# A LayerNorm's mean summed while the convolutions still run, its squares and rstd listed earlier

## The chip, the cores and the metric

The kernel runs on one core of a Trainium2 chip. The metric is the device time of one execution in microseconds (us); lower is better. A core has five engines that run side by side, each through its own fixed list of instructions in order: TensorE (PE, the matmuls; PEld is its weight load), VectorE (DVE), ScalarE (ACT), GpSimd (POOL) and SyncE (SP, which here only issues DMAs).

## The reference, cut to what matters

One layer of a hybrid block, 1024 tokens by 1024 channels, float32. The part that the change touches is mixer B, between the input projection and the merge:

```python
proj = jnp.einsum('bsd,de->bse', h, w_in[l])
b_s, c_s, v_s, v_c, gl_c, gate_br = jnp.split(proj, SPLITS[:-1], axis=-1)
y_a = b_s * causal_dwconv(c_s * v_s, conv_short_w[l])          # mixer A, width 3
y_a = jnp.einsum('bsc,cd->bsd', y_a, w_short_out[l])
u = v_c * jax.nn.sigmoid(gl_c)                                 # mixer B
u = causal_dwconv(u, conv_conf_w[l]) + conv_conf_b[l]          # width 31
u = jax.nn.silu(layer_norm(u, conf_ln_g[l], conf_ln_b[l]))     # mean and variance over channels
y_b = jnp.einsum('bsc,cd->bsd', u, w_conf_out[l])
```

and `layer_norm` is `(u - mean) * rsqrt(mean((u - mean)^2) + 1e-5) * g + b`. Gates, the output projection, a gated feed-forward part and the norms around them follow.

## The kernel before, in words

**Layout.** Activations lie transposed: 8 chunks of 128 channels on the partitions, 1024 tokens along the row, worked on in two halves of 512 (`halves`). A norm over channels is thus a sum over the 8 chunks (elementwise adds) and then a matmul with a 128x128 tile of ones, which sums over the partitions and puts the sum on all of them.

**Precision.** Every matmul operand is split into a high part (`wh`, `zsh`, `q00h`: a cast on ACT) and a low part (`wl`, `zsl`: a subtraction), and `mm3` issues three matmuls for each. The `wl` of the input projection and of `w_short` is made on POOL, that of most others on DVE. PE can only begin a block of weights when its `wl` is there.

**The stages around the change**, in the order of the program text:

1. The input projection ("win stage" below): 12 groups ("duals") of seven products each in the order of `PRODUCTS = "1265734"`. Each product fills PSUM banks named x, y or z, which DVE (`plus`, line 503; `minus_times`, line 507) and ACT read out. `u` chunks, the inputs of the wide convolution, come out of these. The products of the short convolution (`short_conv`, L494 to L496) go through `q_store` (casts `qs` on ACT at L487, subtraction on POOL at L488) to DRAM and come back with `q_load` (L580, SP) in the last dual.
2. The wide convolution `conv(j)`, 8 chunks, all on DVE: two differences (L595, L596), then 46 taps (L604) into two PSUM banks, and ACT's two L617 that add the bias and write the result back over `u[j]`. L618 stores the chunk to `cv_dram`. The calls stand after the win stage in the text, but each tap is tied by `tc.issue_after` to a certain read of a product, so that the convolutions run between the win stage's reads.
3. `y_a`: 8 blocks j of 48 matmuls (`ya`, `col_block`), each read by DVE (L675, which multiplies by a gate that POOL's DMA at L673 fetches), and each followed by one `modulation`, a 128x1024 product-and-sum on DVE (L258) of a row block of `w_ada` that SP loads. After block 1 the text has `ln_mean` and `ln_squares`: the 8 chunks are loaded again (L626, SP), summed on DVE (L628), scaled by 1/1024 (L629), multiplied by ones (`mu`, L632), copied (L633); then per chunk the mean is subtracted (L639), ACT squares (L642), DVE sums (L646). After block 6 it has `ln_rstd`: for each half the `var` matmul (L653), then `rstd`: Ln and Exp on ACT (L323, L324) and a Newton step on DVE (L329 to L331).
4. `y_b`: `row_blocks` over the normalised chunks. `act_b` scales a chunk half (L686), applies Silu (L687), calls a `modulation`, and splits the result (`zsh` L304 on ACT, `zsl` L305 on DVE), which PE takes chunk by chunk.

**What sets the order.** Tiles come from pools with a fixed number of buffers: `uc` (8 wide ones: u, p, sc, qs, sig, cv), `t` (58 of 128x512), `gs` (6), raw weights (5), `wh` and `wl` (3 each), PSUM 6 and 2 banks. A planner turns the text into one fixed list for each engine, by its own estimate of when each instruction can go; among those ready it takes the one listed first. On the chip the lists are then run as they stand, each instruction waiting for its data and for its buffer to come free. An instruction that waits holds all behind it on its engine, a DMA that waits for a buffer holds all behind it on its queue.

Of the kernel before, what the change touches and what calls it, by code (L numbers as in the profile page):

```python
# [34 lines left out]
F32 = mybir.dt.float32  # L35
# [11 lines left out]
SK = 3  # L47
# [58 lines left out]
def block_kernel(ctx: ExitStack, tc: tile.TileContext, xT, c, vecs, ada, w_first, w_plain, w_duals,  # L106
# [41 lines left out]
    def g_tile(name):  # L148
        return gsp.tile([P, H], F32, tag="gs", name=name)
# [168 lines left out]

    def rstd_start(ss, eps, name, n=H, tile_of=g_tile):

        r, t = tile_of(name + "r")[:, :n], tile_of(name + "t")[:, :n]
        ss = ss[:, :n]
        nc.scalar.activation(t, ss, AF.Ln, bias=eps)  # L323
        exp = nc.scalar.activation(r, t, AF.Exp, scale=-0.5)  # L324
        return ss, eps, r, t, exp.ins

    def rstd_end(ss, eps, r, t, exp):

# [1 line left out]
        nc.vector.scalar_tensor_tensor(out=t, in0=ss, scalar=eps, in1=t, op0=ALU.add, op1=ALU.mult)  # L330
        nc.vector.scalar_tensor_tensor(out=r, in0=t, scalar=1.5, in1=r, op0=ALU.add, op1=ALU.mult)  # L331
        return r

    def rstd(*args):
        return rstd_end(*rstd_start(*args))

    def load_ln(ins):

# [170 lines left out]
    def win_evac(pairs):  # L509

        st = [{} for _ in pairs]

        def start(e, kind, j):
            if kind == "u":
                u.append(u_tile(j))
                e["b"] = [u[j][:, CK - 1 + h * H : CK - 1 + (h + 1) * H] for h in range(2)]
            elif kind == "p":
                e["p"] = uc_tile(f"p{j}", T + SK - 1)
                nc.gpsimd.memset(e["p"][:, : SK - 1], 0.0)  # L519
                e["b"] = [e["p"][:, SK - 1 + h * H : SK - 1 + (h + 1) * H] for h in range(2)]  # L520
            elif kind == "g":
                e["t"] = [uc_tile("sig", T) for _ in range(2)]
                e["b"], e["c"] = ([t[:, s] for s in halves] for t in e["t"])

        def evac(i, m, ps):
            kind, j, *rest = pairs[i]
            e = st[i]
            if m == "1":
                start(e, kind, j)
                if kind == "q":  # L530
                    e["b"] = [g_tile("m")]
            if m == "6" and kind == "q":
                e["b"].append(g_tile("v"))
            if m in "16":
                nc.scalar.copy(e["b"][m == "6"], ps)
            elif m in "23":
                h = m == "3"
                b = e["b"][h]
                plus(b, ps, b)
                if kind == "u" and h:  # L540
                    nc.vector.tensor_tensor(b, b, e["z"], ALU.mult)
                elif kind == "p" and h:
                    minus_times(b, e["z"], b)
                elif kind == "q":
                    nc.vector.tensor_tensor(sc[j][:, halves[h]], b, sc[j][:, halves[h]], ALU.mult)
                elif kind == "g":
                    nc.scalar.activation(b, b, AF.Sigmoid)
            elif m == "5":
                e["z"] = e["c"][1] if kind == "g" else g_tile("z")
                nc.scalar.copy(e["z"], ps)  # L550
            elif m == "7":
                plus(e["z"], ps, e["z"])
                if kind in "ug":
                    nc.scalar.activation(e["z"], e["z"], AF.Sigmoid, scale=-1.0)
                elif kind == "q":
                    minus_times(sc[j + 1][:, halves[1]], e["z"], sc[j + 1][:, halves[1]])
            else:
                if kind in "ug":
                    sig = e["c"][0] if kind == "g" else g_tile("sig")
                    nc.scalar.activation(sig, ps, AF.Sigmoid, scale=-1.0)  # L560
                if kind == "u":
                    nc.vector.tensor_tensor(e["b"][0], e["b"][0], sig, ALU.mult)
                elif kind == "p":
                    minus_times(e["b"][0], ps, e["b"][0])
                    short_conv(j, e["p"])
                elif kind == "q":
                    minus_times(sc[j + 1][:, halves[0]], ps, sc[j + 1][:, halves[0]])
                    for i in range(2):
                        q_store(j + i)
                else:  # L570
                    for g, t in zip((j, *rest), e["t"]):
                        nc.scalar.dma_start(gate_dram[g], t)
        return evac
# [15 lines left out]
    def conv(j):  # L589
# [26 lines left out]
        for i, a in enumerate((a0, a1)):  # L616
            nc.scalar.activation(eo[:, : H, i], a, AF.Identity, bias=col(V_CB, j))  # L617
        nc.scalar.dma_start(cv_dram[j], u[j][:, :T])  # L618

    cv = []  # L620

    def ln_mean():
        tot = diffp.tile([P, T + CK - 1], F32, tag="diff", name="tot")[:, :T]
        for j in range(KC):
            cv.append(uc_tile(f"cv{j}", T))
            nc.sync.dma_start(cv[j], cv_dram[j])  # L626
            if j:
                nc.vector.tensor_tensor(tot, tot if j > 1 else cv[0], cv[j], ALU.add)  # L628
        nc.vector.tensor_scalar(tot, tot, 1.0 / D, None, ALU.mult)  # L629
        for h in range(2):  # L630
            mps = ps_tile("mu")
            nc.tensor.matmul(mps, ones, tot[:, halves[h]], start=True, stop=True)  # L632
            nc.scalar.copy(tot[:, halves[h]], mps)  # L633
        return tot

    def ln_squares():
        sqs = [None, None]
        for j in range(KC):
            nc.vector.tensor_tensor(cv[j], cv[j], mu, ALU.subtract)  # L639
            for h in range(2):  # L640
                sq = g_tile("sq")
                nc.scalar.activation(sq, cv[j][:, halves[h]], AF.Square, scale=1.0 / 32.0)  # L642
                if j == 0:
                    sqs[h] = sq
                else:
                    nc.vector.tensor_tensor(sqs[h], sqs[h], sq, ALU.add)  # L646
        return sqs

    def ln_rstd(sqs):
        rl = []  # L650
        for h in range(2):
            vps = ps_tile("var")
            nc.tensor.matmul(vps, ones, sqs[h], start=True, stop=True)  # L653
            rl.append(rstd(vps, eps2, f"rl{h}"))
        return rl

    n_duals = len(PAIRS) // 2
    for d in range(n_duals):
# [11 lines left out]
    for j in range(KC):  # L670
        for h, ps in enumerate(col_block(next_w(), qT, (0, 1), "ya")):
            ga = g_tile("ga")
            nc.gpsimd.dma_start(ga, gate_dram["a", j][:, halves[h]])  # L673
            ma[j, h] = s_tile(f"ma{j}{h}")
            nc.vector.tensor_tensor(ma[j, h], ps, ga, ALU.mult)  # L675
        if j == 1:
            mu = ln_mean()
            sqs = ln_squares()
        if j == 6:
            rl = ln_rstd(sqs)  # L680
        modulation(16 + j)


    def act_b(k, h):
        z = cv[k][:, halves[h]]
        nc.vector.tensor_tensor(z, z, rl[h], ALU.mult)  # L686
        nc.scalar.activation(z, z, AF.Silu, bias=col(V_LNB, k), scale=col(V_LNG, k))  # L687
        modulation(24 + KC * h + k)
        return split(z, s_tile, "zs")

    mg = [[None, None] for _ in range(KC)]

# [397 lines left out]
```

## Time and profile before

| | us |
|---|---|
| median of 3 runs (lowest, highest) | 1544.36 (1543.83, 1546.57) |
| profiled execution, its own time | 1546.12 |
| profiled execution, span of its instructions | 1544.4 |

| engine | busy us in the span | share |
|---|---|---|
| PE | 1472.5 | 95% |
| DVE | 1187.2 | 77% |
| ACT | 639.6 | 41% |
| POOL | 575.9 | 37% |

A timeline row reads: start, duration, engine, line, operation, names written and read, count, and in brackets the engine's idle time before it and what ended that. A row "A <- B: t, n, m" of the waits says that A waited for B t us in all, n times, at most m us. A row of a table of windows gives each engine's busy time in that stretch, with the number of instructions, and then PEclk, the clock that TensorE was granted as a share of full speed, the DMA engines' busy share and GB/s. A row of the groups gives busy us and mean ns, then the idle time before. Buffer numbers are left out of names.

### The profile page before, as it was taken

How to read it: one execution, taken by the hardware profiler on the slowest of the kernel's cores; microseconds unless marked ns; L12 is line 12 of the kernel's file. 1: busy time of each engine (PE TensorE's matmuls, PEld its weight loads, DVE VectorE, ACT ScalarE, POOL GpSimd, SP SyncE). 2: the span in 40 equal slices, each digit the busy share in tenths (PEclk: the TensorE clock that was granted, in tenths of full speed). 3: DMA queues.
4: the chain of work that ended last, by engine and by line, in shares of the span. 5: the costliest groups of instructions: out<-in, count | busy, mean ns of one | idle time of the engine just before them, and what ended most of it. 6: DMA issues, size and time to landing. Idle time of an engine off the chain costs nothing.

```text
span 1544.4 us, 17865 instructions
## 1 busy us (share of the span) xinstructions
PE 1472.5 (95%) x6466; PEld 1208.6 (78%) x6466; DVE 1187.2 (77%) x1543; ACT 639.6 (41%) x896; POOL 575.9 (37%) x491
## 2 busy tenths in 40 slices
PE   5799999999999998989899989999999999999996
PEld 3588887888887887768788868888888888788885
DVE  7887899999998965656865798876767665677756
ACT  6563334333333342344334564444444443221235
POOL 1316778688768883310111101100100016445005
PEclk9999999999999999999999999999999999999998
DMA  9332214223222269455754428544444449999403
GB/s 369 143 100 75 95 55 164 68 96 109 96 82 95 92 230 386 144 184 164 243 191 166 164 82 258 191 150 150 151 150 156 156 151 348 349 308 274 125 14 110
DMA packets 88024, 256.16 MB, mean 166 GB/s; under 512 B 10112, under 2 KB 12288, under 8 KB 87936
## 3 DMA queue, kind: packets, MB, share of 16 engines
q1 hardware_dynamic: 47248, 147.01, 28.5%
q0 software_dynamic: 36944, 95.44, 19.1%
q10 hardware_dynamic: 3744, 12.58, 2.0%
q8 instruction: 50, 0.82, 0.2%
q14 instruction: 38, 0.31, 0.1%
HBM read 188.41 MB, written 66.58 MB: 165 GB/s over the span
## 4 chain that ended last, share of the span: by engine, by line
PE 47%; DVE 3%; issue 1%; ACT 0%; DVEq 0%; ACTq 0%
PE x L276 7%; PE x L273 7%; PE x L274 7%; PE z L273 4%; PE z L274 4%; PE z L276 4%; PE y L273 3%; PE y L276 2%; PE y L274 2%; PE mix L276 2%; PE mix L273 2%; PE mix L274 2%; PE yb L274 1%; PE yb L276 1%; PE yb L273 1%
## 5 line engine op out<-in xcount | busy, mean ns | idle before, releaser
L201 ACT CAST wh<-raw 128x1024 fp32r<-128x1024 f32 (+2 forms) x260 | 262.1, 1009 | 439.5 <-PE x L274 99.7
L202 POOL TENSOR_TENSOR wl<-raw,wh 128x1024 fp32r<-128x1024 f32 (+1 forms) x95 | 247.3, 2608 | 154.5 <-ACT wh L201 149.6
L202 DVE TENSOR_TENSOR wl<-raw,wh 128x1024 fp32r<-128x1024 f32 (+2 forms) x165 | 189.1, 1147 | 58.3 <-ACT wh L201 55.7
L604 DVE SCALAR_TENSOR_TENSOR c<-diff,vec,c 128x512 f32<-128x512 f32 x248 | 182.2, 749 | 3.9
L841 POOL DMA_DIRECT2D hid<-stage x71 | 37.8, 534 | 354.1 <-DVE stage L313 350.9
L273 PE MATMUL x<-th,wh 128*128 128x512 f32 x336 | 130.8, 389 | 0.0
L276 PE MATMUL x<-th,wl 128*128 128x512 f32 x336 | 130.7, 389 | 0.0
L274 PE MATMUL x<-tl,wh 128*128 128x512 f32 x336 | 130.7, 389 | 0.0
L604 DVE SCALAR_TENSOR_TENSOR c<-u,wsum,c 128x512 f32<-128x512 f32 x112 | 84.0, 750 | 2.0
L273 PE MATMUL x<-t2h,wh 128*128 128x512 f32 x184 | 73.8, 402 | 5.9 <-ACT wh L201 4.5
L276 PE MATMUL x<-t2h,wl 128*128 128x512 f32 x184 | 73.8, 402 | 4.7 <-POOL p L519 3.4
L274 PE MATMUL x<-t2l,wh 128*128 128x512 f32 x184 | 73.7, 401 | 0.1
L273 PEld LDWEIGHTS x<-th,wh 128*128 128x128 f32 x336 | 63.1, 188 | 13.2 <-issue 0.3
L274 PEld LDWEIGHTS x<-tl,wh 128*128 128x128 f32 x336 | 63.1, 188 | 13.2
L276 PEld LDWEIGHTS x<-th,wl 128*128 128x128 f32 x336 | 63.1, 188 | 13.1
L273 PE MATMUL z<-th,wh 128*128 128x512 f32 x168 | 65.4, 389 | 1.5 <-ACT wh L201 1.5
L258 DVE CUSTOM_DVE_ANT_0 raw<-raw,cs,vec 128x1024 f32<-128x1024 f32 x24 | 30.7, 1281 | 45.7 <-DMA raw<-in_ada 45.7
L276 PE MATMUL z<-th,wl 128*128 128x512 f32 x168 | 65.4, 389 | 0.0
L274 PE MATMUL z<-tl,wh 128*128 128x512 f32 x168 | 65.4, 389 | 0.0
L312 ACT CAST stage<-g 128x512 fp32r<-128x512 f32 x62 | 38.3, 620 | 56.5 <-DMA hid<-stage 29.3
L273 PE MATMUL yb<-zsh,wh 128*128 128x512 f32 x128 | 49.5, 400 | 10.4 <-ACT zsh L304 9.4
L313 DVE TENSOR_TENSOR stage<-g,stage 128x512 fp32r<-128x512 f32 x62 | 42.5, 688 | 20.0 <-ACT stage L312 20.0
(819 smaller groups left out, 4087.5 us busy)
## 6 DMA issues: line engine op xcount, KB each, us to landing
hid<-stage POOLq DMA_DIRECT2D x71, 512.0 KB, 4.3
raw<-in_w_fi SPq DMA_DIRECT2D x50, 512.0 KB, 4.3
raw<-in_w_duals SPq DMA_DIRECT2D x48, 512.0 KB, 3.5
th<-hid POOLq DMA_DIRECT2D x71, 256.0 KB, 6.1
tl<-hid POOLq DMA_DIRECT2D x71, 256.0 KB, 6.3
ada<-in_ada SPq DMA_DIRECT2D x24, 512.0 KB, 7.5
raw<-in_ada SPq DMA_DIRECT2D x24, 512.0 KB, 4.3
raw<-in_w_fo SPq DMA_DIRECT2D x24, 384.0 KB, 6.1
```

Of the source, the lines that this page charges most:

```text
L201: nc.scalar.copy(wh, raw)
L202: lo_engine.tensor_tensor(wl, raw, f32(wh), ALU.subtract)
L258: nc.vector.tensor_tensor_reduce(out=raw, in0=raw, in1=cs, scale=1.0, scalar=col(V_ADA, b), op0=ALU.mult, op1=ALU.add, accum_out=modc(b),)
L273: nc.tensor.matmul(ps, wh, xh, start=first, stop=False, skip_group_check=again)
L274: nc.tensor.matmul(ps, wh, xl, start=False, stop=False, skip_group_check=again)
L276: mm3.ins = nc.tensor.matmul(ps, wl, xh, start=False, stop=last, skip_group_check=again).ins
L312: nc.scalar.copy(hi, src)
L313: nc.vector.tensor_tensor(lo, src, f32(hi), ALU.subtract)
L604: nc.vector.scalar_tensor_tensor(out=out, in0=src[:, s : s + H], scalar=wt, in1=acc, op0=ALU.mult, op1=ALU.add)
L841: nc.gpsimd.dma_start(hid_dram[key], s)
```

## The change

The sum over chunks is no longer made from the reloaded chunks. Two accumulators `tot` of 128x512 are taken from pool `t` and cleared on POOL ahead of the win stage; each `conv(j)` ends with two DVE additions that add the finished chunk's halves to them. `ln_mean` is now only two matmuls with ones and two ACT copies that carry the factor 1/1024. The reloads of the chunks stand in `ln_squares`, whose subtraction goes by halves. `ln_mean` and `ln_squares` are listed after block 0 of `y_a` rather than block 1, `ln_rstd` after block 5 rather than block 6, and within `ln_rstd` both `var` matmuls come first, then both Ln, then both Exp. In `act_b` the split stands ahead of the `modulation`. The clearing of the two leading columns of `p` moves from POOL to DVE.

```diff
@@ -318,11 +318,14 @@
 
     def rstd_start(ss, eps, name, n=H, tile_of=g_tile):
 
-        r, t = tile_of(name + "r")[:, :n], tile_of(name + "t")[:, :n]
+        t = tile_of(name + "t")[:, :n]
         ss = ss[:, :n]
         nc.scalar.activation(t, ss, AF.Ln, bias=eps)
-        exp = nc.scalar.activation(r, t, AF.Exp, scale=-0.5)
-        return ss, eps, r, t, exp.ins
+        return ss, eps, *exp_half(t, name, n, tile_of)
+
+    def exp_half(t, name, n=H, tile_of=g_tile):
+        r = tile_of(name + "r")[:, :n]
+        return r, t, nc.scalar.activation(r, t, AF.Exp, scale=-0.5).ins
 
     def rstd_end(ss, eps, r, t, exp):
 
@@ -330,9 +333,6 @@
         nc.vector.scalar_tensor_tensor(out=t, in0=ss, scalar=eps, in1=t, op0=ALU.add, op1=ALU.mult)
         nc.vector.scalar_tensor_tensor(out=r, in0=t, scalar=1.5, in1=r, op0=ALU.add, op1=ALU.mult)
         return r
-
-    def rstd(*args):
-        return rstd_end(*rstd_start(*args))
 
     def load_ln(ins):
 
@@ -516,7 +516,7 @@
                 e["b"] = [u[j][:, CK - 1 + h * H : CK - 1 + (h + 1) * H] for h in range(2)]
             elif kind == "p":
                 e["p"] = uc_tile(f"p{j}", T + SK - 1)
-                nc.gpsimd.memset(e["p"][:, : SK - 1], 0.0)
+                nc.vector.memset(e["p"][:, : SK - 1], 0.0)
                 e["b"] = [e["p"][:, SK - 1 + h * H : SK - 1 + (h + 1) * H] for h in range(2)]
             elif kind == "g":
                 e["t"] = [uc_tile("sig", T) for _ in range(2)]
@@ -616,28 +616,30 @@
         for i, a in enumerate((a0, a1)):
             nc.scalar.activation(eo[:, : H, i], a, AF.Identity, bias=col(V_CB, j))
         nc.scalar.dma_start(cv_dram[j], u[j][:, :T])
+        for h in range(2):
+            nc.vector.tensor_tensor(tot[h], tot[h], u[j][:, halves[h]], ALU.add)
 
     cv = []
+    tot = [hl_tile(f"tot{h}", dt=F32) for h in range(2)]
+    for t in tot:
+        nc.gpsimd.memset(t, 0.0)
 
     def ln_mean():
-        tot = diffp.tile([P, T + CK - 1], F32, tag="diff", name="tot")[:, :T]
+        mu = []
+        for h in range(2):
+            mps = ps_tile("mu")
+            nc.tensor.matmul(mps, ones, tot[h], start=True, stop=True)
+            nc.scalar.activation(tot[h], mps, AF.Copy, scale=1.0 / D)
+            mu.append(tot[h])
+        return mu
+
+    def ln_squares():
+        sqs = [None, None]
         for j in range(KC):
             cv.append(uc_tile(f"cv{j}", T))
             nc.sync.dma_start(cv[j], cv_dram[j])
-            if j:
-                nc.vector.tensor_tensor(tot, tot if j > 1 else cv[0], cv[j], ALU.add)
-        nc.vector.tensor_scalar(tot, tot, 1.0 / D, None, ALU.mult)
-        for h in range(2):
-            mps = ps_tile("mu")
-            nc.tensor.matmul(mps, ones, tot[:, halves[h]], start=True, stop=True)
-            nc.scalar.copy(tot[:, halves[h]], mps)
-        return tot
-
-    def ln_squares():
-        sqs = [None, None]
-        for j in range(KC):
-            nc.vector.tensor_tensor(cv[j], cv[j], mu, ALU.subtract)
             for h in range(2):
+                nc.vector.tensor_tensor(cv[j][:, halves[h]], cv[j][:, halves[h]], mu[h], ALU.subtract)
                 sq = g_tile("sq")
                 nc.scalar.activation(sq, cv[j][:, halves[h]], AF.Square, scale=1.0 / 32.0)
                 if j == 0:
@@ -647,12 +649,14 @@
         return sqs
 
     def ln_rstd(sqs):
-        rl = []
+        vs, ts = [], []
         for h in range(2):
-            vps = ps_tile("var")
-            nc.tensor.matmul(vps, ones, sqs[h], start=True, stop=True)
-            rl.append(rstd(vps, eps2, f"rl{h}"))
-        return rl
+            vs.append(ps_tile("var"))
+            nc.tensor.matmul(vs[h], ones, sqs[h], start=True, stop=True)
+        for h in range(2):
+            ts.append(g_tile(f"rl{h}t"))
+            nc.scalar.activation(ts[h], vs[h], AF.Ln, bias=eps2)
+        return [rstd_end(vs[h], eps2, *exp_half(ts[h], f"rl{h}")) for h in range(2)]
 
     n_duals = len(PAIRS) // 2
     for d in range(n_duals):
@@ -673,10 +677,10 @@
             nc.gpsimd.dma_start(ga, gate_dram["a", j][:, halves[h]])
             ma[j, h] = s_tile(f"ma{j}{h}")
             nc.vector.tensor_tensor(ma[j, h], ps, ga, ALU.mult)
-        if j == 1:
+        if j == 0:
             mu = ln_mean()
             sqs = ln_squares()
-        if j == 6:
+        if j == 5:
             rl = ln_rstd(sqs)
         modulation(16 + j)
 
@@ -685,8 +689,9 @@
         z = cv[k][:, halves[h]]
         nc.vector.tensor_tensor(z, z, rl[h], ALU.mult)
         nc.scalar.activation(z, z, AF.Silu, bias=col(V_LNB, k), scale=col(V_LNG, k))
+        hl = split(z, s_tile, "zs")
         modulation(24 + KC * h + k)
-        return split(z, s_tile, "zs")
+        return hl
 
     mg = [[None, None] for _ in range(KC)]
 
```

## The prediction

> **What bounds the kernel now.** The page first, for the busiest engine.
>
> ```profile
> span 1544.4 us, 17865 instructions
> PE 1472.5 (95%) x6466; PEld 1208.6 (78%) x6466; DVE 1187.2 (77%) x1543; ACT 639.6 (41%) x896; POOL 575.9 (37%) x491
> ```
>
> PE is busy in 1472.5 of 1544.4 us, so an edit that removes no matmul can win at most the 71.9 us in which PE stands, plus what it loses at a lowered clock after standing. The next view is therefore PE's own waits, and of these the ones that the edited code can touch:
>
> ```profile
> PE yb L273 <- ACT zsh L304: 9.4, 2, 7.4
> PE mu L632 <- DVE tot L629: 4.8, 1, 4.8
> PE x L276 <- POOL p L519: 3.4, 1, 3.4
> ```
>
> The timeline shows the first two in place, one in the middle of `y_a` and one at its end:
>
> ```profile
> 588.18 16.15 SPq L626 DMA_DIRECT2D cv<-cv  x8
> 590.42 0.39 PE L273 MATMUL ya<-q00h,wh 128*128 128x512 f32 x1
> 601.30 0.39 PE L273 MATMUL ya<-q00h,wh 128*128 128x512 f32 x1
> 611.84 1.22 DVE L628 TENSOR_TENSOR tot<-tot,cv 128x1024 f32<-128x1024 f32 x1
> 614.18 2.82 DVE L629 TENSOR_SCALAR tot<-tot 128x1024 f32<-128x1024 f32 x1
> 617.14 3.49 PE L632 MATMUL mu<-tot,ones 128*128 128x512 f32 x4 [4.80 <-DVE tot L629]
> 674.92 1.88 PE L653 MATMUL var<-sq,ones 128*128 128x512 f32 x4
> 681.87 1.28 ACT L323 ACT_TABLE_LOAD   x1 [2.18 <-issue]
> 694.40 0.61 ACT L304 CAST zsh<-cv 128x512 fp32r<-128x512 f32 x1
> 695.06 2.08 PE L273 MATMUL yb<-zsh,wh 128*128 128x512 f32 x4 [7.37 <-ACT zsh L304]
> ```
>
> A block of `y_a` takes 601.30 - 590.42 = 10.88 us. After block 1 PE comes to `mu` at 612.3 and waits 4.80 us for the sum, whose chunks were still being loaded up to 604. After block 7 it waits 7.37 us for the first normalised chunk, because `var` was computed only one block earlier and the chain from there to `yb` took 695.06 - 674.92 = 20.1 us. Both waits are followed by a slower clock:
>
> ```profile
> 200.00:300.00 100.00, 98.97 (x437) 81.65 (x436) 96.85 (x125) 39.35 (x54) 76.51 (x35) 1.00 0.31 101
> 300.00:400.00 100.00, 100.00 (x443) 82.84 (x442) 96.20 (x120) 40.95 (x55) 83.43 (x39) 1.00 0.28 101
> 400.00:500.00 100.00, 96.15 (x411) 78.68 (x411) 91.81 (x119) 34.54 (x46) 70.08 (x33) 0.97 0.27 94
> 617.14:620.70 3.56, 3.56 (x6) 1.66 (x7) 3.47 (x6) 0.62 (x2) 0.00 (x0) 0.57 0.45 115
> 695.06:699.10 4.04, 4.04 (x10) 3.23 (x11) 4.04 (x6) 3.45 (x6) 0.72 (x2) 0.54 0.63 162
> ```
>
> In the last two rows PE works at 0.57 and 0.54 of its clock: 3.56 x 0.43 = 1.53 us and 4.04 x 0.46 = 1.86 us are lost there. The first three rows are the win stage, and the price of the change: DVE, fifth column, is busy 96.85, 96.20 and 91.81 of 100 us, and that is where the sums now go.
>
> **The change part by part.**
>
> *The mean.* The last of the eight convolutions ends 20 us before `y_a` begins, as the stores show, which follow one another at (569.6 - 189.9) / 7 = 54 us, and DVE stands for 10 us after it:
>
> ```profile
> L618 ACTq DMA_DIRECT2D cv<-u x8: 326/326/327, 189.9 to 569.6; - x8
> 577.07 0.69 DVE L503 TENSOR_TENSOR sig<-x,sig 128x512 f32<-128x512 f32 x1 [10.18 <-issue]
> ```
>
> So `tot` is there by about 575, and `mu` after block 0 finds it ready: gain 4.80 + 1.53 = 6.33 us. The two `mu` matmuls stay, and the factor 1/1024 rides on copies that were there already. DVE loses seven 1024-wide additions and L629 from `y_a`; that was on PE's path only through the wait just counted, so nothing more is added for it.
>
> *Squares.* Eight subtractions of 1.2 us become sixteen of about 0.6: nothing. They wait for `mu` and the reloads. The reloads stand earlier in the text by one block, past the weight and `ada` loads of that block on SP's queue, but they were issued from 588.18 already and then took 16.15 us because they waited for `uc` buffers; the buffers come free as before, so SP stays held until about 604, and the weights behind it are as late as before. The squares ended so:
>
> ```profile
> 620.67 0.59 ACT L633 COPY tot<-mu 128x512 f32<-128x512 f32 x1 [0.86 <-PE mu L632]
> 648.81 1.29 DVE L258 CUSTOM_DVE_ANT_0 raw<-raw,cs,vec 128x1024 f32<-128x1024 f32 x1 [6.59 <-DMA raw<-in_ada]
> 650.02 1.29 DVE L646 TENSOR_TENSOR sq<-sq 128x512 f32<-128x512 f32 x2
> ```
>
> that is, at 651.3, 30 us after `mu`'s copies. Counted from the last reload, some 5 us after its issue near 604, they now end near 640.
>
> *rstd.* `var` after block 5 leaves blocks 6 and 7, 21.8 us, to cover the chain of 20.1 us, and the chain is shorter: two of its four table loads go (1.28 us each), and so does the 2.18 us before the second Ln, as both Ln now follow one another. With about 15 us of chain against 21.8 the wait of 7.37 goes, with its clock: 9.23 us. Next late is the other wait of `yb` on `zsh`, 9.4 - 7.4 = 2.0 us, which lies later in the stage and is not counted as won. If the cover of two blocks were lost, this term is what is paid again.
>
> *Split ahead of `modulation`* moves 0.6 us of DVE forward of 1.3 us in a stage where both fit: nothing. *Two more tiles of `t`* during the win stage: 56 of 58 are held by operands, so the loads of `q` may come up to two tiles later, at 3 matmuls or 10.88 / 16 = 0.68 us each. *The clearing of `p`* goes off POOL and onto DVE.
>
> ```profile
> 584.09 0.32 SPq L580 DMA_DIRECT2D q71l<-q  x1
> L519 POOL MEMSET p<- x8: 95/101/104, 58.2 to 484.5; 128x2 f32 x8
> ```
>
> The last `q` was issued at 584.09 and is used at the end of block 0, 600: nothing. The clearing is 0.1 us eight times, small beside the lag counted next.
>
> Gain so far: 6.33 + 9.23 = 15.56 us.
>
> *The sixteen additions.* This is the cost, and the trace has no such addition. The nearest rows are DVE's other two-input operations, both inputs in SBUF, of this width:
>
> ```profile
> 638.60 2.49 DVE L646 TENSOR_TENSOR sq<-sq 128x512 f32<-128x512 f32 x4
> L595 DVE TENSOR_TENSOR diff<-u 128x527 f32<-128x527 f32 x8 | 9.2, 1153 | 0.1
> L596 DVE TENSOR_TENSOR diff<-u 128x526 f32<-128x526 f32 x8 | 10.5, 1312 | 0.0
> L562 DVE TENSOR_TENSOR u<-u,sig 128x512 f32<-128x512 f32 x5 | 10.5, 2096 | 0.0
> L562 DVE TENSOR_TENSOR u<-u,sig x5: 680/2875/2884, 209.5 to 518.8; 128x512 f32<-128x512 f32 x5
> ```
>
> Outside the win stage one takes 2.49 / 4 = 0.62 us; inside it 1.15 and 1.31 us on average, and at worst 2.88. I take 1.23, the mean of L595 and L596, since they too are two in a row on `u`, at the start of each convolution as the additions are at its end. Bounds: 0.62 and 2.88.
>
> By the Trainium skill, page "SBUF — State Buffer", section "Who interferes with whom", a DVE instruction with two SBUF inputs and a POOL instruction that reads SBUF exclude each other, and the second waits for the whole of the first. That speaks against moving additions to where POOL is busiest. Worked out with POOL busy about 0.77 of the time in operations of 2.4 us (an estimate from that page), an addition would cost 0.62 + 0.77 x 1.2 = 1.55 us, and the median would come out at 1538.5 instead of the 1535.3 below.
>
> What is late by it? DVE's lists leave it little to catch up in:
>
> ```profile
> 265.23 0.69 DVE L503 TENSOR_TENSOR z<-x,z 128x512 f32<-128x512 f32 x1 [1.95 <-PE x L276]
> 341.39 0.69 DVE L503 TENSOR_TENSOR z<-x,z 128x512 f32<-128x512 f32 x1 [2.06 <-PE x L276]
> 417.55 0.69 DVE L503 TENSOR_TENSOR z<-x,z 128x512 f32<-128x512 f32 x1 [1.74 <-PE x L276]
> 500.93 0.69 DVE L503 TENSOR_TENSOR z<-x,z 128x512 f32<-128x512 f32 x1 [6.28 <-PE x L276]
> ```
>
> At 54 us each from 189.9 on, five convolutions have ended by 417. Their ten additions take 12.3 us against 1.95 + 2.06 + 1.74 = 5.75, so DVE reaches the end of the sixth 6.5 us later than before. The last six additions lie ahead of or among 6.28 and 10.18 us of slack and are hidden. A late DVE does not stop PE by itself, but at one place it does so through a queue:
>
> ```profile
> 456.72 0.73 ACT L617 ACTIVATE u<-c,vec 128x512 f32<-128x512 f32 x1 [6.00 <-DVE c L604]
> 457.33 1.03 ACT L201 CAST wh<-raw 128x1024 fp32r<-128x1024 f32 x1
> 458.44 2.40 POOL L202 TENSOR_TENSOR wl<-raw,wh 128x1024 fp32r<-128x1024 f32 x1 [5.11 <-ACT wh L201]
> 482.22 2.35 POOL L202 TENSOR_TENSOR wl<-raw,wh 128x1024 fp32r<-128x1024 f32 x1
> 484.62 0.79 PE L276 MATMUL x<-t2h,wl 128*128 128x512 f32 x1 [3.36 <-POOL p L519]
> ```
>
> ACT waits for the sixth convolution's last tap; the weight cast behind it on ACT waits too; POOL waits for the cast and then works without a break to 484.57, where PE has waited 3.36 us for that `wl` (the page puts it to the clearing of `p`, which ran beside it at 484.5). What DVE is late at 456.7 is late at 484.6: cost 6.5 us. Bounds: at 0.62 an addition, 6.2 - 5.75 = 0.5 us; at 2.88, 28.8 - 5.75 = 23.0 us. The additions also wait for ACT's second L617, 0.73 us, which the planner can fill with the next convolution's differences.
>
> Sum: -15.56 + 6.5 = -9.1 us. The profiled execution of 1546.12 would become 1537.1; the median of the runs lies 1.76 lower, 1544.36, and becomes 1535.3.
>
> **The rivals.**
>
> *Full gain.* The additions fall where POOL is idle or are spread by the planner, and cost what they cost outside: -15.56 + 0.5, 1529.3. For it: POOL is idle a quarter of the win stage, and a wait of 1.74 to 2.06 us comes with every second dual. Against it: the averages of L595 and L596.
>
> *Slower, by the additions.* If each meets a POOL operation as three of the five L562 did, the ten cost 28.8 us and the lag at 456.7 is 23.0 us: -15.56 + 23.0 = +7.5, 1551.8. It decides from (15.56 + 5.75) / 10 = 2.13 us per addition. For it: the 2.88 itself, POOL at 83.43 of 100 us in one window, and that a second addition right behind a first would find POOL waiting. Against it: L595 and L596 are such pairs and stay at 1.2. The page named above makes this same mechanism.
>
> *The wait at the end of `y_a` comes back.* If the planner lists the squares or `var` later than the text suggests, or if the gate loads of L673, which share the six `gs` tiles with the squares, hold up `y_a`'s PSUM banks, 9.23 us return: -6.33 + 6.5, within 0.2 us of 1544.4. For it: the 6.59 us above, in which DVE waited on an `ada` load with squares left to sum. Against it: 17 us lie between 640 and `var` after block 5, at 590.4 + 6 x 10.88 + 1.3 for `mu` = 657.
>
> **How the numbers follow.** Forecast case, a gain of some 4 to 13 us: 0.50. Full gain 0.22. Return of the wait 0.08. Slower by the additions 0.20. A measurement of this kernel can tell about 0.2%, 3.1 us: faster is the first two, 0.72; same is the third, 0.08; slower 0.20. The range runs from 1527, the full gain and the 2.0 us of `yb`'s other wait, up to 1549, an addition of 2.6 us; beyond them lie about 2 in 10. The likeliest case alone spans 1531 to 1541.
>
> **What would show it.** Right: no wait before `mu` nor before the first `yb`, the clock at 1.00 in both places, two blocks between `var` and `yb`, table loads down by two, L628 and L629 gone, sixteen additions in the win stage of 0.7 to 2 us, and PE's wait for `wl` after the ninth dual longer than 3.36. Wrong: additions of over 2.1 us or PE waits in the win stage of over 20 us in all; or the end of `y_a` still waiting on `zsh`; or new waits of PE on DVE's reads, which this kernel does not have in the win stage.

## The result, and the profile after

| | before, us | after, us |
|---|---|---|
| median (lowest, highest) | 1544.09 (1543.37, 1546.57) | 1559.74 (1557.17, 1563.87) |
| span of the profiled execution | 1544.4 | 1558.7 |
| `y_a` begins | 590.4 | 599.8 |
| first `yb` matmul | 695.1 | 708.7 |

The changed kernel is slower: the ratio of the times is 1.0101, 95% interval 1.0076 to 1.0126. Forecast was 1535.3, a gain of 9.1 us. In the profiled executions 9.4 us are lost before `y_a` begins and another 4.3 from there to the first `yb`; `y_b` loses 3.3 more, and later stages give 2.7 back; these two were not followed further.

The page of the changed kernel, for the engines, and then PE's waits that the change can touch:

```profile
span 1558.7 us, 17886 instructions
PE 1480.1 (95%) x6466; PEld 1212.5 (78%) x6466; DVE 1203.5 (77%) x1567; ACT 635.3 (41%) x894; POOL 578.0 (37%) x485
```

```profile
PE yb L273 <- ACT zsh L304: 8.1, 2, 6.1
PE ya L273 <- DVE ma L679: 7.1, 2, 4.7
PE x L276 <- POOL wl L202: 4.0, 3, 1.8
```

PE does the same 6466 matmuls in 7.6 us more; its mean granted clock is 0.982 instead of 0.986. The wait for `mu` is gone. The wait before the first `yb` fell only from 7.37 to 6.14. In the win stage the waits of x for `wl` grew from 1.0 us, once, to 4.0 in three, and small waits for reads by ACT and DVE are new; new too is the wait of `y_a` for its own read-outs. The timeline of the changed kernel shows where, the win stage first:

```profile
223.89 0.50 PE L273 MATMUL x<-th,wh 128*128 128x512 f32 x1 [1.39 <-ACT v L535]
238.98 0.50 PE L273 MATMUL x<-th,wh 128*128 128x512 f32 x1 [1.19 <-DVE sig L503]
255.05 0.50 PE L276 MATMUL x<-t2h,wl 128*128 128x512 f32 x1 [1.69 <-POOL wl L202]
371.41 0.50 PE L276 MATMUL x<-t2h,wl 128*128 128x512 f32 x1 [1.79 <-POOL wl L202]
485.88 0.50 PE L276 MATMUL y<-h40h,wl 128*128 128x512 f32 x1 [1.34 <-POOL wl L202]
495.12 0.51 PE L276 MATMUL x<-t2h,wl 128*128 128x512 f32 x1 [3.50 <-POOL u L405]
```

The last of these is the wait of 3.36 us that the kernel before has at 484.62, hardly longer; the others were 1.03 us (the third), 0.5 (the fifth) or nothing there. Between 180 and 500 us PE waits 12.0 us instead of 4.9. Then `y_a` and the first `yb`:

```profile
599.79 0.39 PE L273 MATMUL ya<-q00h,wh 128*128 128x512 f32 x1
610.68 1.88 PE L631 MATMUL mu<-tot,ones 128*128 128x512 f32 x4
649.92 0.77 PE L273 MATMUL ya<-q00h,wh 128*128 128x512 f32 x1 [4.71 <-DVE ma L679]
678.83 0.47 PE L273 MATMUL ya<-q00h,wh 128*128 128x512 f32 x1 [2.36 <-DVE ma L679]
708.69 3.36 PE L273 MATMUL yb<-zsh,wh 128*128 128x512 f32 x7 [6.14 <-ACT zsh L304]
```

`mu` has no bracket: it found its input. A `ya` matmul that waits for `ma` waits for a PSUM bank: the halves of three blocks fill the six banks, and the fourth cannot begin before the first is read out. Each of the three bracketed waits here is followed by a stretch at half clock, PEclk 0.50 in this table of windows:

```profile
649.10:655.90 6.80, 5.98 (x14) 4.77 (x15) 6.06 (x9) 1.04 (x1) 5.68 (x6) 0.50 0.92 317
679.80:683.20 3.40, 3.40 (x10) 2.62 (x9) 0.16 (x1) 1.50 (x3) 0.00 (x0) 0.50 0.67 267
707.10:713.90 6.80, 5.21 (x12) 4.18 (x13) 5.17 (x9) 3.62 (x7) 0.90 (x2) 0.50 0.73 225
```

So up to the first `yb` the stage pays 4.71 + 2.36 in waits and about 3.0 + 1.7 in clock (half of what PE worked in the first two windows), and wins 6.33 at `mu` and 1.23 at `yb`: 11.8 - 7.6 = 4.2 us, about the loss seen.

### The profile page after: what moved, and what is told of

Its sections match the earlier page's. It is cut to its first block, busy times and chain, and to the rows that moved or that the text cites. A ratio compares the mean times of both kernels' runs of the same rounds, so it can differ in the third digit from the quotient of the medians.

```text
span 1558.7 us, 17886 instructions
## 1 busy us (share of the span) xinstructions
PE 1480.1 (95%) x6466; PEld 1212.5 (78%) x6466; DVE 1203.5 (77%) x1567; ACT 635.3 (41%) x894; POOL 578.0 (37%) x485
## 4 chain that ended last, share of the span: by engine, by line
PE 46%; DVE 3%; issue 1%; ACT 0%; DVEq 0%; ACTq 0%
PE x L276 7%; PE x L274 7%; PE x L273 7%; PE z L274 3%; PE z L273 3%; PE z L276 3%; PE y L273 2%; PE y L274 2%; PE y L276 2%; PE mix L276 2%; PE mix L273 2%; PE mix L274 2%; PE yb L273 1%; PE yb L274 1%; PE yb L276 1%
## 5 line engine op out<-in xcount | busy, mean ns | idle before, releaser
L276 PEld LDWEIGHTS x<-th,wl 128*128 128x128 f32 x336 | 63.1, 188 | 14.1 <-POOL wl L202 1.0
L258 DVE CUSTOM_DVE_ANT_0 raw<-raw,cs,vec 128x1024 f32<-128x1024 f32 x24 | 35.5, 1482 | 42.0 <-DMA raw<-in_ada 30.5
```

The source lines that it names most:

```text
L258: nc.vector.tensor_tensor_reduce(out=raw, in0=raw, in1=cs, scale=1.0, scalar=col(V_ADA, b), op0=ALU.mult, op1=ALU.add, accum_out=modc(b),)
L276: mm3.ins = nc.tensor.matmul(ps, wl, xh, start=False, stop=last, skip_group_check=again).ins
```

## The experiments

Three theories came out of the two traces. **A**: the additions make DVE late in the win stage, and with it ACT's casts, POOL's `wl` and PE. **B**: listing reloads and squares after block 0 keeps `y_a`'s read-outs waiting; at first I took the gate loads behind the squares' `gs` tiles as the cause. **C**: the wait before the first `yb` is not the rstd chain, but that the split takes its tile from pool `t`, whose tiles are handed out in the order of the text, so that it can't be placed ahead of the last `ma` of `y_a`. The rival to B and C is the prediction's own: the chain from `var` to `yb`. All times are medians; the kernel before ran beside each group at 1543.0 to 1543.9.

| run | edit | median, us | ratio to before (95%) | `y_a` begins | first `yb` |
|---|---|---|---|---|---|
| a_noadds | after, no additions | 1548.40 | 1.0033 (1.0020, 1.0045) | 590.0 | 698.7 |
| a_wide | after, wide additions | 1555.37 | 1.0077 (1.0057, 1.0096) | 595.8 | 703.9 |
| a_pooladds | after, additions on POOL | 1556.12 | 1.0080 (1.0065, 1.0095) | 596.9 | 706.8 |
| a_poolms | after, `p` cleared on POOL | 1562.77 | 1.0120 (1.0095, 1.0145) | 604.5 | 713.6 |
| a_sq1 | after, reloads and squares after block 1 | 1543.69 | 1.0003 (0.9987, 1.0020) | 598.4 | 692.9 |
| a_rel0 | after, squares alone after block 1 | 1557.00 | 1.0093 (1.0070, 1.0116) | 599.6 | 706.7 |
| a_sq1_r6 | a_sq1, rstd after block 6 | 1540.89 | 0.9984 (0.9974, 0.9993) | 599.2 | 692.2 |
| a_z0 | after, own tile for chunk 0's split | 1554.08 | 1.0061 (1.0039, 1.0084) | 599.7 | 701.6 |
| b_z0 | before, own tile | 1538.63 | 0.9973 (0.9958, 0.9988) | 590.9 | 689.2 |
| a_sq1_z0 | a_sq1, own tile | 1538.25 | 0.9965 (0.9954, 0.9976) | 597.5 | 688.0 |
| b_z0_j2 | b_z0, mean and squares after block 2 | 1532.92 | 0.9925 (0.9910, 0.9940) | 590.0 | 682.0 |
| n_sum2 | after without additions, and the findings | 1533.60 | 0.9930 (0.9913, 0.9947) | 589.0 | 681.9 |

**The additions (A).** The first run takes them out and leaves `tot` cleared.

```diff
-        for h in range(2):
-            nc.vector.tensor_tensor(tot[h], tot[h], u[j][:, halves[h]], ALU.add)
```

> After, without the sixteen additions: the accumulators keep their zeros, so the mean is left out of the LayerNorm. Theory A (the additions meet POOL's operations, 1.73 us each, DVE falls behind and PE pays in the win stage): y_a begins near 590 instead of 599.8, the stage's PE gaps shrink to those of before (1.0, 0.5, 3.4 us), and the time falls by about 9.5 us, to 1550. Rival (the planner's new order and the clearing of p on DVE cost it): y_a still begins near 599 and the time stays within 3 us of 1559.7. Neither expects y_a itself to change: 4.7, 2.4 and 6.1 us of gaps stay.

1548.4: 11.3 us come back, and `y_a` begins at 590.0, where the kernel before has 590.4. The additions are the cost of the win stage. Theory A named ACT's casts and POOL's `wl` as the way to PE; the lines above show waits for reads by ACT and DVE as well. The waits behind the win stage remain, `y_a`'s own (5.11 and 2.63 us) and the one before `yb`, which grew to 8.19 us, so the rest of the loss is another matter. Next, one addition of double width instead of two:

```diff
-        for h in range(2):
-            nc.vector.tensor_tensor(tot[h], tot[h], u[j][:, halves[h]], ALU.add)
+        nc.vector.tensor_tensor(totw, totw, u[j][:, :T], ALU.add)
```

> The changed kernel with one addition of 128x1024 at the end of each convolution instead of two of 128x512, on an accumulator of that width; since SBUF is full, the pool of 128x512 tiles has 57 buffers instead of 58. In the changed kernel an addition of 128x512 took 0.68 us at best and 1.73 on average, 2.90 at most. If the difference is a wait that each instruction pays once (for a POOL operation under way), a wide one takes 1.2 us of its own (L628 of before, 1.22) and about 1.05 of waiting, 2.3 in all, the first five 11.5 instead of 15.5, and y_a begins some 4 us sooner, near 596 us; the time falls by about 4 us, to 1555 or 1556. If DVE simply works at a lower rate there, a wide one takes 3.4 us and neither y_a's start nor the time moves. One tile of the pool less can cost up to some us elsewhere, so the start of y_a decides, not the median.

The groups of the changed kernel and of this one (busy us, mean ns), then their rows by tile (min/median/max ns):

```profile
L620 DVE TENSOR_TENSOR tot<-tot,u 128x512 f32<-128x512 f32 x16 | 27.2, 1730 | 0.8 <-ACT u L617 0.8
L620 DVE TENSOR_TENSOR tot<-tot,u x16: 675/2032/2898, 191.4 to 577.6; 128x512 f32<-128x512 f32 x16
```

```profile
L619 DVE TENSOR_TENSOR tot<-tot,u 128x1024 f32<-128x1024 f32 x8 | 14.0, 1756 | 0.8 <-ACT u L617 0.8
L619 DVE TENSOR_TENSOR tot<-tot,u x8: 1211/1222/2827, 192.9 to 572.3; 128x1024 f32<-128x1024 f32 x8
```

Twice the width takes the same mean time, the best case goes from 0.68 to 1.21, and five of the eight wide ones take no more than 1.23: what is paid above the work itself is a wait per instruction, not a lower rate. The timeline shows what is waited for. Each of the nine additions of the changed kernel that took over 1.7 us ends 0.55 us after the POOL instruction that was under way; the one of 2.28 us at 358.99, for example, after POOL's `wl` of 357.87 to 360.72. `y_a` begins 4.0 us sooner, as expected, and the median falls by 4.4. But the first five wide additions took 8.8 us, not the expected 11.5, against 15.5 for the ten narrow ones: of 6.8 us less on DVE only 4.0 arrive at `y_a`. Then the additions on POOL:

```diff
-            nc.vector.tensor_tensor(tot[h], tot[h], u[j][:, halves[h]], ALU.add)
+            nc.gpsimd.tensor_tensor(tot[h], tot[h], u[j][:, halves[h]], ALU.add)
```

> The changed kernel with the sixteen additions issued on POOL instead of DVE. POOL's own 128x512 subtraction with two inputs (L488) took 1.48 us on average in the win stage, so sixteen are some 22 us, on an engine that is busy about 78 of 100 us there. If what costs is only that DVE is late (lag at the sixth convolution, then ACT, the weight cast, POOL's wl and PE), the lag goes and POOL takes the additions into its idle time, but for one or two that fall into its stretch without a break at 458 to 484 us: y_a begins near 592 us and the time is near 1552. Rival: POOL's idle time is waiting for casts and no slack, each addition makes the wl behind it late by its length, and DVE's two-input operations wait for POOL instead: y_a begins at 600 us or later and the time is 1560 or more.

```profile
L620 POOL TENSOR_TENSOR tot<-tot,u 128x512 f32<-128x512 f32 x16 | 25.7, 1625 | 14.6 <-ACT u L617 14.6
```

Neither number was met: `y_a` begins at 596.9, between the two expectations. POOL carries 25.7 us of additions and stands 14.6 us ahead of them for ACT's L617; `y_a` begins 6.9 us later than without additions. Neither engine of the two has them for nothing. Last, the clearing of `p` back on POOL:

```diff
-                nc.vector.memset(e["p"][:, : SK - 1], 0.0)
+                nc.gpsimd.memset(e["p"][:, : SK - 1], 0.0)
```

> The changed kernel with the clearing of p back on POOL: this takes out that part alone. On DVE the eight clearings took 0.06 us each, one of them after a wait of 1.01 us for a DMA that stores a gate. Theory (the part costs nothing): 1558 to 1561, no difference that can be told. Rival (a clearing that waits on DVE for its buffer holds all behind it, just where DVE is late): 1 to 3 us faster, and the waits of PE near 255 and 371 us shorter.

```profile
L620 DVE TENSOR_TENSOR tot<-tot,u 128x512 f32<-128x512 f32 x16 | 31.6, 2005 | 0.8 <-ACT u L617 0.8
```

Against 27.2 us in the changed kernel: two more additions met a POOL operation (2.9 us instead of 0.68), and `y_a` begins 4.7 us later. The medians can't be told apart (1557.63 to 1566.06 here, 1557.17 to 1563.87 there). The price of an addition thus hangs on where in POOL's work it falls, which an edit of 0.06 us instructions moves by some us.

**Reloads and squares (B).** Both listed after block 1, the mean still after block 0:

```diff
         if j == 0:
             mu = ln_mean()
+        if j == 1:
             sqs = ln_squares()
```

> After, with the reloads and squares listed after block 1 of y_a again, the mean still after block 0. Theory B (the gate loads of block 1 stand behind the squares' tiles, so blocks 1 to 3 fill the six PSUM banks and block 4 waits): the gap of 4.71 us ahead of block 4 and the half clock behind it (3.0 us) go, the time falls by 5 to 8 us, to about 1553. Rival (POOL's slow weight operation of 10.8 us is what holds the banks, whatever the place of the squares): the gap stays at 3 us or more.

1543.69, 16 us less, twice what I had expected: both waits of `ya` went, with their half clocks, and the wait before `yb` fell to 3.68. The place in the text is what costs, but this edit moves two things. The last run parts them: the reloads stay after block 0, the squares alone go after block 1.

```diff
         if j == 0:
             mu = ln_mean()
+            ln_reload()
         if j == 1:
             sqs = ln_squares()
```

> The changed kernel with the squares listed after block 1 (as in the run in which reloads and squares were both listed there, 1543.69 us), but with the eight reloads still listed after block 0, as the changed kernel has them. This parts the two things that moved together: the reloads' place on SP's queue and the squares' place on DVE, ACT and POOL. If the reloads are the cause (ahead of one ada and one w_short load they hold SP until 615 us; DVE stands for the ada load, ACT for the weights, the second copy of mu comes at 622.9 and the squares begin at 621.9), the squares begin near 622 again, run without a break, PE waits for read-outs of y_a about 4 us or more, and the time is 1552 to 1560. If the squares' place is the cause (ahead of the gate loads and the read-out of block 1), the read-out of block 1 comes before them, PE finds banks, and the time is 1543 to 1547. Anything between 1547 and 1552 means that both count.

1557.0, `y_a`'s wait is 6.6 us, now in one piece, ahead of block 6, where the changed kernel has the second of its two:

```profile
635.57 1.28 DVE L682 TENSOR_TENSOR ma<-ya,ga 128x512 f32<-128x512 f32 x2
674.46 1.28 DVE L258 CUSTOM_DVE_ANT_0 raw<-raw,cs,vec 128x1024 f32<-128x1024 f32 x1 [3.52 <-DMA raw<-in_ada]
675.67 1.28 DVE L682 TENSOR_TENSOR ma<-ya,ga 128x512 f32<-128x512 f32 x2
676.50 0.77 PE L273 MATMUL ya<-q00h,wh 128*128 128x512 f32 x1 [6.63 <-DVE ma L682]
```

So about 13 of the 16 us are the reloads' place on SP's queue, and my first reading of B, the gate loads behind the squares, explains at most the other 2.7. What the reloads do in the changed kernel is in the timelines. Before:

```profile
584.77 1.32 SPq L189 DMA_DIRECT2D raw<-in_w_short  x2
586.15 0.42 SPq L189 DMA_DIRECT2D raw<-in_ada  x1
587.50 0.33 SPq L189 DMA_DIRECT2D raw<-in_w_short  x1
588.18 16.15 SPq L626 DMA_DIRECT2D cv<-cv  x8
604.39 0.43 SPq L189 DMA_DIRECT2D raw<-in_ada  x1
```

After:

```profile
595.48 1.18 SPq L189 DMA_DIRECT2D raw<-in_w_short  x2
598.17 16.79 SPq L640 DMA_DIRECT2D cv<-cv  x8
615.01 0.42 SPq L189 DMA_DIRECT2D raw<-in_ada  x1
615.49 0.42 SPq L189 DMA_DIRECT2D raw<-in_w_short  x1
...
620.72 1.29 DVE L258 CUSTOM_DVE_ANT_0 raw<-raw,cs,vec 128x1024 f32<-128x1024 f32 x1 [8.79 <-issue]
621.93 1.29 DVE L642 TENSOR_TENSOR cv<-cv,tot 128x512 f32<-128x512 f32 x2
621.96 1.05 ACT L201 CAST wh<-raw 128x1024 fp32r<-128x1024 f32 x1 [9.62 <-DMA raw<-in_w_short]
622.92 0.59 ACT L632 ACTIVATE tot<-mu 128x512 f32<-128x512 f32 x1
633.79 10.76 POOL L202 TENSOR_TENSOR wl<-raw,wh 128x1024 fp32r<-128x1024 f32 x1 [8.30 <-ACT wh L201]
644.49 2.15 POOL L677 DMA_DIRECT2D ga<-gate_a  x4
649.08 1.34 DVE L679 TENSOR_TENSOR ma<-ya,ga 128x512 f32<-128x512 f32 x2 [3.45 <-DMA ga<-gate_a]
```

One `ada` load and one weight load that stood ahead of the eight reloads stand behind them now, and the reloads hold SP for 16.79 us while `uc` buffers come free. DVE stands 8.79 us before a `modulation`, whose `ada` row was asked for only at 615.01 (the bracket says no more than "issue"), ACT 9.62 us at the cast of that weight, and the second copy of `mu` is listed behind the cast. So the squares begin at 621.93, though `mu` was multiplied at 610.68. They then run with one break of 0.3 us, DVE busy 20.08 of 20.40 us (621.9 to 642.3), nearly all two-input operations; POOL's next `wl`, 2.40 us elsewhere, takes 10.76 and ends 2.3 us after them; the gate load behind it on POOL goes out at 644.49, and block 1 is read out at 649.08, after PE has filled all banks. In a_sq1, with the two loads ahead again, the squares begin at 611.0, block 1 is read out in the midst of them, at 623.87, and POOL's `wl` that begins beside this read-out takes 2.41 us. How much the 10.76 us of POOL and how much the `gs` tiles add to the chain was not parted. In a_rel0 the late loads cost about as much by another way: block 1 is read out at 635.57 without a wait of PE, and PE stands ahead of block 6, for a read-out that DVE has listed behind a `modulation` whose `ada` row came late (3.52 us). So the two runs show the price of the reloads' place; the chain down to block 1 is the reading of one trace.

**The first `yb` (C).** One tile of pool `diff`, free at that time, for chunk 0's split; after and before:

```diff
-        hl = split(z, s_tile, "zs")
+        hl = split(z, first_z if h == 0 and k == 0 else s_tile, "zs")
```

> After, with the split of y_b's first chunk in a tile of its own (the buffer of the differences, free by then) instead of two tiles of pool t. Theory C (tiles of t are handed out in the order of the text, so no split can be placed ahead of the read-out of y_a's last block; that, not the rstd chain, is what y_b's first matmul waits for): the gap of 6.14 us at the end of y_a shrinks to under 1.5 us and its half clock (2.6 us) goes, the time falls by 6 to 9 us, to about 1552. Rival (the prediction's: the chain from var through Ln, Exp and Newton is too long): the gap stays near 6 us, within 1.5.

> Before, with the split of y_b's first chunk in a tile of its own. Theory C: the gap of 7.37 us shrinks to what the rstd chain leaves, which in before ends about 2 us after y_a's last block (rl0r done at 687.1, first Silu at 689.2 against 687.7), so to 2 to 4 us; the time falls by 4 to 7 us, to about 1538.5. Rival (chain): the gap stays at 6 us or more, the time within 2 us of 1544.1.

1554.08 and 1538.63: 5.7 and 5.3 us less, the first just short of the 6 to 9 expected. In the changed kernel first, then with the tile:

```profile
689.49 0.68 DVE L334 SCALAR_TENSOR_TENSOR rl0r<-rl0t,rl0r 128x512 f32<-128x512 f32 x1
...
705.95 1.28 DVE L679 TENSOR_TENSOR ma<-ya,ga 128x512 f32<-128x512 f32 x2
708.03 2.69 ACT L304 CAST zsh<-cv 128x512 fp32r<-128x512 f32 x5
```

```profile
688.87 0.69 DVE L334 SCALAR_TENSOR_TENSOR rl0r<-rl0t,rl0r 128x512 f32<-128x512 f32 x1
...
692.23 0.61 ACT L304 CAST zs<-cv 128x512 fp32r<-128x512 f32 x1
694.89 1.29 DVE L679 TENSOR_TENSOR ma<-ya,ga 128x512 f32<-128x512 f32 x2
```

Without the tile, rstd is done at 690.2 and the split still comes at 708.0, 0.8 us after the last read-out, with all sixteen Silus ahead of it on ACT; with it, the split comes 3 us after rstd, ahead of the read-outs of the last two blocks, and PE does not wait at the first `yb`. (It waits 2.32 us at 706.79 instead, for a read-out of `y_a`.) In b_z0 the wait of 7.37 us becomes one of 1.97. That the pool's order is the cause was tried only by this way around it. The rival is tested by taking the earlier rstd away from a_sq1:

```diff
-        if j == 5:
+        if j == 6:
             rl = ln_rstd(sqs)
```

> The changed kernel with the reloads and squares listed after block 1 (as in the run with that edit alone, 1543.69 us), and rstd listed after block 6 instead of block 5. This takes away the earlier rstd alone. By the prediction's step, in which the chain of 20 us from var to yb is what yb waits for, the wait before the first yb grows from 3.7 us to 10 or more: 1550 to 1555. By the theory that the last read-out of y_a must come before the first split, because both take tiles of one pool in the order of the text, rstd one block later costs nothing or little: the wait of yb stays between 3 and 8 us and the time between 1543 and 1548.

1540.89: a block less of cover, and it is 2.8 us faster in the medians, faster than either expectation. The wait before `yb` is 2.41 us instead of 3.68:

```profile
691.00 1.28 DVE L679 TENSOR_TENSOR ma<-ya,ga 128x512 f32<-128x512 f32 x2
691.58 0.61 ACT L304 CAST zsh<-cv 128x512 fp32r<-128x512 f32 x1
692.24 2.82 PE L273 MATMUL yb<-zsh,wh 128*128 128x512 f32 x7 [2.41 <-ACT zsh L304]
```

The rival falls. With rstd early, ACT had sixteen Silus ahead of the split, and the split came at 692.27; here it has four, and the split comes at 691.58, although the last read-out is 0.8 us later (691.00 instead of 690.18).

**Put together.** First a_sq1 and the own tile, both edits as above. Then before with the own tile and this:

```diff
-        if j == 1:
+        if j == 2:
             mu = ln_mean()
             sqs = ln_squares()
```

And a new version, the changed kernel without additions, with `p` cleared on POOL, the own tile, and the sum from the reloaded chunks (`ln_sum`: the loads and seven additions, as before):

```diff
-        if j == 0:
+        if j == 1:
+            tot = ln_sum()
+        if j == 2:
             mu = ln_mean()
             sqs = ln_squares()
-        if j == 5:
+        if j == 6:
             rl = ln_rstd(sqs)
```

> The changed kernel with the reloads and squares listed after block 1 and with the split of chunk 0 in a tile of its own. By the two theories together (gate loads behind the squares' tiles; first split behind y_a's last read-out) the 3.68 us before the first yb and the half clock after it, 691.4 for 6.8 us, go on top of what the first edit gave: 1543.7 - 4 to - 6 = 1538 to 1540, and what is left over before's version with that edit (1538.6) is the additions' 9.5 us less the mean's 6.3. By the rival that the rstd chain is the bound, the wait before the first yb stays near 3.7 us and the time at 1543 to 1544.

> The kernel before, with two edits: the split of chunk 0 of y_b goes into a tile of its own (as in the run of before with that edit alone, 1538.63 us), and mean and squares are listed after block 2 of y_a rather than after block 1. Theory (the mean waits for the reloads, which end near 604 us, and nothing but that): one block more, 10.9 us, covers the 4.80 us wait of mu and its 1.5 us of half clock, and since the squares then end near 660 us and var comes after block 6, near 668 us, nothing new is late: 1538.6 - 6.3 = 1532. The gate loads stand behind the squares' gs tiles one block later, but the block is covered by the 6 banks only if the squares go as fast as before: if they hold y_a's banks as they did in the changed kernel (4.71 and 2.36 us), the gain is used up: 1538 to 1540. Rival (the rstd chain must have its 20 us): squares that end 11 us later push var and the first yb back by about as much: 1540 to 1545, with a wait of yb on rstd's Newton step or on var.

> A version put together from the findings: no additions in the win stage and the clearing of p on POOL, as before; the chunks reloaded and summed after block 1 of y_a, mean and squares after block 2 (factor 1/1024 on the copies of mu, subtraction by halves), rstd after block 6 with both Ln ahead of both Exp, the split ahead of the modulation, and chunk 0's split in a tile of its own. If the additions were the cost of the win stage, the squares' gate loads the cost of y_a and the tile order the wait before yb, all three are gone and so is mu's wait: y_a begins at 590, mu and the first yb find their inputs, 1528 to 1533. If the squares, now ending one block later, hold up the gate loads or var: 1535 to 1542.

1538.25, 1532.92 and 1533.60: the first as the theories gave it, the other two 0.9 and 0.6 us above. In the second PE no longer waits for `mu` or for `ma`:

```profile
PE yb L273 <- ACT zsh L304: 2.0, 1, 2.0
PE yb L273 <- DVE gb L713: 1.8, 2, 1.6
PE yb L273 <- ACT zs L304: 1.4, 1, 1.4
```

It beats both kernels, before by 10.4 us. The third has more of the change in it (the paired Ln and Exp, the factor on the copies, the halves, the order in `act_b`) and is no faster: those parts together are worth nothing that can be measured here.

## Why the prediction was wrong

- *The mean ready early*: right. `mu` found its input and kept its clock. But b_z0_j2 gets the same by listing the old sum one block later, and pays nothing for it.
- *The additions*: the cost is theirs, but its place was wrong and its size too small, 9.4 us instead of 6.5. The step that failed is the way to PE. The prediction let the lag reach PE in one place alone, in the wait for `wl` after the ninth dual: "What DVE is late at 456.7 is late at 484.6". That wait hardly grew, from 3.36 to 3.50 us. PE lost its time ahead of it, from 223.89 on, in five waits of 1.2 to 1.8 us, and by the half clock behind that of 1.79. Two of the five are waits for reads by ACT and DVE, so "A late DVE does not stop PE by itself" was wrong as well; the prediction's own list has such waits among the signs of being wrong. As to the size, I took 1.23 us for one addition, from the means of L595 and L596; the first ten took 15.54 us, five of them 0.68 each and five 1.78 to 2.90. With these the prediction's sum for DVE's lag, 15.5 - 5.75 = 9.8 us, holds: the sixth convolution ends 9.9 us later (L617 on ACT at 466.60 instead of 456.72). In a_poolms the ten took 20.0 us, the sum gives 14.2, and `y_a` begins 14.1 us later than before. In a_wide it does not hold, 8.8 - 5.75 = 3.0 against 5.4 us, and why stays open.
- The estimate from the Trainium skill, page "SBUF — State Buffer", section "Who interferes with whom", was 1.55 us for an addition: here the page was nearer than the rows I chose. Its rule, that the second instruction waits for the whole of the first, agrees with the nine slow additions, which all end 0.55 us after the POOL instruction under way. That its figure is also the mean of the first ten is luck: in a_poolms the same ten took 2.0 us each.
- *Squares: nothing*: this step failed, and in it the sentence on the reloads, "the weights behind it are as late as before". I saw that they move past a weight and an `ada` load on SP's queue, and then priced the queue's hold, not the two loads that would now stand behind it, nor who waits for them. They cost about 13 us (a_rel0 against a_sq1). The squares did end near 640, at 642.3; that was of no use, since nothing waited for them.
- *rstd*: this step failed too. I counted 7.37 + 1.86 us to the chain because `var` stood 20.1 us ahead of `yb`; of the wait 1.23 us went. That two things follow each other in this distance does not show that one bounds the other. Two more rows of the kernel before had the answer:

```profile
688.42 0.81 ACT L687 ACTIVATE cv<-cv,vec 128x512 f32<-128x512 f32 x1 [1.32 <-DVE cv L686]
693.73 1.28 DVE L675 TENSOR_TENSOR ma<-ya,ga 128x512 f32<-128x512 f32 x2
```

The chain ends with this first Silu, at 689.23. The split of the same chunk comes only at 694.40, behind four more Silus and a weight cast on ACT and just after the first of the last two read-outs. The place of the split in the list was the bound, and a tile of its own took the wait down to 1.97 us (b_z0).
- *The rivals*: "slower, by the additions" had the right sign by luck. It asked for 2.88 us an addition, and over 2.13 to be slower at all; the ten took 1.55 on average, and the kernel is slower because of the reloads and the gain at `yb` that did not come. "The wait comes back" named `y_a`'s banks, but through gate loads, and I weighed it by the time left to `var`, not by the time until block 1 is read out.
- By these measures the sum is: additions +9.4, reloads and what follows in `y_a` +11.8, mean -6.3, `yb` -1.2, together +13.7 of the 14.3 us between the two profiled executions; a slower `y_b` and what later stages give back make the rest. The range did not hold it because no case in it joined two costs.

## What to carry to other kernels

When a step with DMAs in it is moved, list what each queue does in the new order, and price the loads that fall behind the moved ones through their readers, down to the instructions listed behind those. Before a wait is put down to a long chain, look at what its engine did just before: here the split's input was ready 5 us before the split, and giving it a tile of its own won 5 us where starting the chain earlier won nothing. Work taken off one stage lands in another; the sixteen sums, 0.68 us each when nothing is in the way, took 1.73 on average beside a busy POOL.

## What the runs showed of the hardware

- A DVE addition of two SBUF operands, 128x512, took 0.68 or up to 2.90 us in one and the same stage; one of 128x1024 took 1.21 or up to 2.83. The slow narrow ones of the changed kernel all end 0.55 us after a POOL instruction, the slow wide ones 1.08 or 1.09.
- It goes the other way too: while DVE ran such operations one behind the other, a POOL subtraction of 2.40 us took 10.76. I had counted only POOL's hold on DVE.
- A wait of PE of 2.36 us was followed by 3.40 us at half clock, so that it cost 1.7 us more than it shows. One of 1.79 us was enough: behind it (371.41) PEclk is 0.57 from 372 to 376 us. Behind those of 1.39 and 1.69 us it stayed at 1.00.
